# Start of a hybrid decoder block on one core: order of the first loads, of the token scaling and of the first two projection tiles

## Chip, cores and metric

The kernel runs on one core of a Trainium2 chip. The metric is device time in microseconds for one launch; the times of before are three runs. Beside them there is one profiled execution, from which every row below comes. The engines are named as in the profile: PE (TensorE matmul), PEld (its weight load), DVE (VectorE), ACT (ScalarE), POOL (GpSimd) and SP (SyncE, which here only issues DMAs).

## What is computed

16 meta tokens and 256 tokens of width 1024 are layer-normed and projected by `w_in` (1024 x 5640). The columns feed a gated delta net (four heads), a stick-breaking attention (eight heads) and two gates; their outputs are merged, projected, added to the residual and normed; then comes a mixture of 32 experts (one group of four, two experts in it) and a last norm. All of it is float32.

```python
h = layer_norm(jnp.concatenate([meta, x], axis=1), ln_emb_g, ln_emb_b)
proj = h @ w_in                      # (272, 5640)
dn_qkv, dn_z, dn_b, dn_a, sb_qkv, gates = jnp.split(proj, SPLIT_POINTS, axis=-1)
dn_qkv = silu(causal_depthwise_conv(dn_qkv, dn_conv_w))
mix = (sig(gA) * (gated_delta_rule(...) @ w_branch_dn)
       + sig(gB) * (stick_breaking(...) @ w_branch_sb)) @ w_out
h = layer_norm(DEEPNORM_ALPHA * h + mix, ln1_g, ln1_b)
h = layer_norm(DEEPNORM_ALPHA * h + hierarchical_moe(h, ...), ln2_g, ln2_b)
return h[:, N_META:]
```

## The kernel before

**Start of the program.** The meta tokens go to tile `xm` (16 x 1024), the 256 tokens to tile `h1` in two halves of 128 rows (`xt[0]` and `xt[1]`, called first half and second half below; the profile calls both `h`). SP issues these three loads (L112, L113, L115); ACT issues five small parameter loads into `rows` (L114 to L119). While they travel PE runs five matmuls on zeros (L185). For each of the three pieces `norm_stats` (L165) runs two BN_STATS on DVE, then `row_stats` (L172) a BN_AGGR on DVE and two small operations on POOL, an addition and a power (L176, L177), whose result is the row's scale. After all three come three scalings on DVE (L191), in place. Then PE transposes the pieces (L208), 128 columns (one chunk) at a time; each chunk becomes `hf` (272 columns, L211 on ACT or L214 on DVE), a rounded copy `hTh` (L212 on DVE or L215 on ACT) and the rest `hTl` (L216 on DVE). There are eight chunks.

**Projection.** `w_in` is taken in 44 tiles of 128 columns. `load_split` (L224) loads one tile (512 KB, SP, L230) into one of three raw buffers, ACT rounds it (`A.copy`, L231), and POOL, or DVE for three of the tiles, subtracts (L232). Three tiles are kept split (`WB`), and three raw (`WR`). A product is three matmuls (`mm3`, L236 to L238) for each of the eight chunks: high weights by `hTh`, high weights by `hTl`, low weights by `hTh`; the last needs POOL's result.

```python
            c, n0, use, j = todo[i]
            wh, wl = split[i]
            pt = ps("sb" if i % 2 and i < 16 else "acc", f"pj{c}")
            for k in range(KT):
                mm3(pt[:, n0:L], wh[:, k, :], wl[:, k, :], hTh[:, k, n0:], hTl[:, k, n0:], k == 0, k == KT - 1)
            use(pt, j)
```

The first four tiles (columns 512, 640, 768 and 896) are keys: `use` is `conv_use`, ACT's L309, three DVE operations (L311) and ACT's L312. After the fourth tile comes a narrow product `pba`, from which the gating of the delta net is computed on DVE (L417 to L442); PE needs its result at L445.

**What sets the order.** On PE, ACT, DVE and SP a scheduler of the tile framework orders the instructions from their dependences; POOL alone keeps the order in which the code is written (`manual_schedule`). DMAs share eight completion semaphores per kind in turn, so that a DMA also waits until the one that had its semaphore before has landed (the names `DMAHW0` to `DMAHW7` below).

Of the kernel before, what the change touches and what calls it, by code (L numbers as in the profile page):

```python
# [7 lines left out]
F32 = mybir.dt.float32  # L8
# [9 lines left out]
P = 128  # L18
D = 1024
KT = 8  # L20
NM = 16
NT = 256
L = NM + NT
# [13 lines left out]
WR = 3  # L37
# [40 lines left out]
def block_kernel(ctx: ExitStack, tc: tile.TileContext, io, out, dbg=None):  # L78
    nc = tc.nc
    V, A, G, T, S = nc.vector, nc.scalar, nc.gpsimd, nc.tensor, nc.sync  # L80
# [8 lines left out]
    def ps(tag, name):  # L89
        return psp.tile([P, 512], F32, tag=tag, bufs=PB[tag], name=name)  # L90
# [15 lines left out]


# [3 lines left out]
    rows = x0.tile([P, P], F32, name="rows")  # L111
    S.dma_start(xm, io["meta_tokens"])  # L112
    S.dma_start(xt[0], io["x"][:P, :])  # L113
    A.dma_start(rows[0:8, :], io["ln_emb_g"].rearrange("(r p) -> r p", p=P))  # L114
    S.dma_start(xt[1], io["x"][P:, :])  # L115
    A.dma_start(rows[8:16, :], io["ln_emb_b"].rearrange("(r p) -> r p", p=P))
    A.dma_start(rows[16:64, :], io["dn_conv_w"].rearrange("j (r p) -> (j r) p", p=P))
# [68 lines left out]
    xstat = {}  # L186
    for i, xa, n in ((2, xm, NM), (0, xt[0], P), (1, xt[1], P)):
        xstat[i] = norm_stats(xa, n, f"e{i}")
    for i, xa, n in ((2, xm, NM), (0, xt[0], P), (1, xt[1], P)):
        mv, r = xstat[i]  # L190
        V.tensor_scalar(xa[:n], xa[:n], mv[:n, 0:1], r[:n], op0=ALU.subtract, op1=ALU.mult)  # L191
# [30 lines left out]
    wring = []  # L222

    def load_split(src, name, pool=None, bufs=WB, sub=None):  # L224
        a, b = src.shape[1:]
        wring.append(name)
        raw = lt.tile([P, 1024], F32, name=f"wr_{name}", tag=f"wr{len(wring) % WR}").rearrange("p (a b) -> p a b", a=a)
        both = (pool or rg).tile([P, 2048], F32R, name=f"ws_{name}", tag="rd", bufs=bufs)
        wh, wl = (both[:, i * 1024:(i + 1) * 1024].rearrange("p (a b) -> p a b", a=a) for i in range(2))
        S.dma_start(raw, src)  # L230
        A.copy(wh, raw)  # L231
        (sub or V).tensor_sub(wl, raw, f32(wh))  # L232
        return wh, wl
# [6 lines left out]
    w_in = io["w_in"].rearrange("(k p) c -> p k c", p=P)  # L240
# [5 lines left out]
    def project(n):  # L246

        for _ in range(n):
# [4 lines left out]
            c, n0, use, j = todo[i]  # L253
            wh, wl = split[i]
            pt = ps("sb" if i % 2 and i < 16 else "acc", f"pj{c}")
            for k in range(KT):
                mm3(pt[:, n0:L], wh[:, k, :], wl[:, k, :], hTh[:, k, n0:], hTl[:, k, n0:], k == 0, k == KT - 1)
            use(pt, j)
# [1277 lines left out]
```

## Time and profile before

| | us |
|---|---|
| three runs: lowest, median, highest | 559.96, 560.81, 561.68 |
| the profiled execution: own time | 558.53 |
| its span, first to last instruction | 556.8 |
| busy in the span: PE, DVE, ACT, POOL | 475.9, 232.7, 185.0, 171.1 |
| mean granted TensorE clock over the span | 0.937 of full speed |

A span view gives for each engine the time in which it ran something, not the time in which others waited for it. A timeline row gives an instruction's start, its duration, its source line and, in brackets, how long its engine had been idle before it and which event ended that. A duration includes any time that an instruction, once started, was held up.

### The profile page before, as it was taken

To read this page: it belongs to the slowest core of one execution; us is meant where nothing else is said; L and a number is where in the kernel's file an instruction comes from. 1 tells how busy PE (TensorE), PEld (TensorE's weight loads), DVE (VectorE), ACT (ScalarE), POOL (GpSimd) and SP (SyncE) were. 2 spreads that over 40 slices of the span, in tenths; PEclk is the share of its full clock that TensorE was granted. 3 is DMA by queue.
4 is the path that set the end of the run, shared out by engine and by line. 5 is a ranking of instruction groups with operands and counts; after the bars stand their busy time and mean duration, and the time that the engine had idled before them with its cause. 6 is when DMAs were issued, how large, how long until landed. Compare 5 with 4: busy or idle time off the path is not lost. (4 is left out here: it accounts for less than half of the span.)

```text
span 556.8 us, 8809 instructions
## 1 busy us (share of the span) xinstructions
PE 475.9 (85%) x3353; PEld 339.4 (61%) x3353; DVE 232.7 (42%) x516; ACT 185.0 (33%) x382; POOL 171.1 (31%) x154
## 2 busy tenths in 40 slices
PE   7898799999998998999799879886879898468681
PEld 4797788899987876789787755441222233222520
DVE  5785825663245433336995756220120101001016
ACT  2554345446545464444353412120210201101100
POOL 7492886745544355445450300000000000000002
PEclk9698999999999999999999899897999788879796
DMA  8553242233432414339879995999999999999922
GB/s 202 122 141 87 64 120 82 78 89 101 126 103 75 112 43 117 111 99 316 285 276 416 406 395 207 419 417 419 419 420 417 422 419 415 421 403 421 414 115 75
DMA packets 74582, 136.35 MB, mean 245 GB/s; under 512 B 9857, under 2 KB 59154, under 8 KB 62242
## 3 DMA queue, kind: packets, MB, share of 16 engines
q1 hardware_dynamic: 72640, 134.26, 65.5%
q10 hardware_dynamic: 1890, 1.39, 0.7%
q8 instruction: 33, 0.54, 0.4%
q14 instruction: 19, 0.16, 0.1%
HBM read 133.54 MB, written 2.10 MB: 244 GB/s over the span
## 5 line engine op out<-in xcount | busy, mean ns | idle before, releaser
L232 POOL TENSOR_TENSOR ws_in<-wr_in,ws_in 128x1024 fp32r<-128x1024 f32 x41 | 99.1, 2421 | 74.4 <-ACT ws_in L231 71.5
L236 PE MATMUL pj<-hTh,ws_in 128*128 128x256 f32 (+1 forms) x352 | 105.9, 302 | 1.7 <-ACT hTh L215 1.0
L238 PE MATMUL pj<-hTh,ws_in 128*128 128x256 f32 (+1 forms) x352 | 102.5, 292 | 0.0
L237 PE MATMUL pj<-hTl,ws_in 128*128 128x256 f32 (+1 forms) x352 | 102.2, 292 | 0.2 <-DVE hTl L216 0.2
L1273 PE MATMUL pg<-gu,xs 128*32 128x512 f32 x640 | 76.0, 604 | 11.1 <-DMA gu<-expert_w_up 7.7
L1493 POOL TENSOR_SCALAR rs<-mv 128x1 f32<-128x1 f32 x2 | 0.4, 221 | 233.4 <-DVE mv L1492 233.4
L236 PEld LDWEIGHTS pj<-hTh,ws_in 128*128 128x128 f32 x352 | 68.1, 194 | 4.0 <-issue 1.4
L237 PEld LDWEIGHTS pj<-hTl,ws_in 128*128 128x128 f32 x352 | 67.8, 193 | 1.5 <-issue 0.9
L238 PEld LDWEIGHTS pj<-hTh,ws_in 128*128 128x128 f32 x352 | 67.6, 192 | 0.8 <-issue 0.7
L1273 PEld LDWEIGHTS pg<-gu,xs 128*32 128x32 f32 x640 | 32.4, 111 | 50.3 <-issue 44.4
L1322 PE MATMUL py<-dn,hd 128*32 128x512 f32 x320 | 46.8, 717 | 12.8 <-DMA dn<-expert_w_down 7.8
L231 ACT CAST ws_in<-wr_in 128x1024 fp32r<-128x1024 f32 x44 | 45.9, 1042 | 3.1 <-DMA wr_in<-w_in 3.1
L1298 DVE TENSOR_SCALAR sc<-pt,smod 128x256 fp32r<-128x256 f32 x10 | 4.8, 484 | 99.0 <-PE pt L1297 99.0
L1326 DVE TENSOR_TENSOR yy<-py,yy 128x512 fp32r<-128x512 f32 x20 | 13.8, 692 | 63.6 <-ACT yy L1325 56.5
L1322 PEld LDWEIGHTS py<-dn,hd 128*32 128x32 f32 x320 | 10.9, 126 | 39.8 <-issue 24.2
L1334 PE MATMUL y<-yy,sc 128*128 128x512 f32 x80 | 25.8, 439 | 4.3 <-ACT yy L1325 3.0
L1304 ACT ACTIVATE gs<-pg 128x256 f32<-128x256 f32 x10 | 3.8, 384 | 76.4 <-PE pg L1273 76.4
L1334 PEld LDWEIGHTS y<-yy,sc 128*128 128x128 f32 x80 | 13.9, 194 | 21.9 <-ACT yy L1325 7.4
L1325 ACT CAST yy<-py 128x512 fp32r<-128x512 f32 x20 | 11.7, 586 | 45.5 <-PE py L1322 44.4
L729 DVE TENSOR_TENSOR_SCAN kp<-kp,one 128x144 f32<-128x144 f32 (+1 forms) x16 | 17.5, 1125 | 14.8 <-ACT kp L724 14.8
L311 DVE SCALAR_TENSOR_TENSOR qkv<-pj,cols,qkv 128x271 f32<-128x271 f32 (+2 forms) x36 | 17.8, 498 | 12.9 <-ACT qkv L309 12.3
L888 POOL TENSOR_TENSOR h<-h,gb 128x512 f32<-128x512 f32 x8 | 12.9, 1645 | 12.9 <-ACT gb L885 12.9
(539 smaller groups left out, 830.1 us busy)
## 6 DMA issues: line engine op xcount, KB each, us to landing
gu<-expert_w_gate SPq DMA_DIRECT2D x32, 1024.0 KB
gu<-expert_w_up SPq DMA_DIRECT2D x32, 1024.0 KB
dn<-expert_w_down SPq DMA_DIRECT2D x32, 1024.0 KB
wr_in<-w_in SPq DMA_DIRECT2D x44, 512.0 KB
wr_o<-w_out SPq DMA_DIRECT2D x8, 512.0 KB
wr_w_branch_dn<-w_branch_dn SPq DMA_DIRECT2D x4, 512.0 KB
wr_w_branch_sb<-w_branch_sb SPq DMA_DIRECT2D x4, 512.0 KB
h<-x SPq DMA_DIRECT2D x2, 512.0 KB
```

The source lines that it names most:

```text
L231: A.copy(wh, raw)
L232: (sub or V).tensor_sub(wl, raw, f32(wh))
L236: T.matmul(pt, lh, rh, start=first, stop=False)
L237: T.matmul(pt, lh, rl, start=False, stop=False)
L238: T.matmul(pt, ll, rh, start=False, stop=last)
L311: V.scalar_tensor_tensor(y[:, s:], pt[:, :L - s], ccol(3 - s, r + j), y[:, s:], op0=ALU.mult, op1=ALU.add)
L729: V.tensor_tensor_scan(k_, k_, bc(one1, [P, n]), 1.0, op0=ALU.mult, op1=ALU.mult)
L888: G.tensor_tensor(x_, x_, gb, op=op)
L1273: T.matmul(pgd[u, part][c, :], xsd[u, part][:, k, c], raw[e][0][:, :, k, :], start=k == 0, stop=k == KT - 1)
L1322: T.matmul(py[c, :], hd[(u + part) % 2][:, r, c], raw[e][1][:, r, n * 512:(n + 1) * 512], start=r == 0, stop=r == 1)
L1326: V.tensor_sub(yy[:, 1, :], py, f32(yy[:, 0, :]))
L1334: T.matmul(y[t][n], sct[(u + part) % 2][:, t * P:(t + 1) * P], yy[:, p_, :], start=False, stop=p_ == 1 and part == 0 and u == NQ - 1)
```

## The change

The loads of the first three `w_in` tiles are written ahead of three of the small parameter loads (`prefetch`), with `raw_weights` split off from `load_split`. The order of SP's first loads becomes first half of the tokens, meta tokens, second half. The scaling of each piece is written directly behind its own statistics. The first two tiles of the projection are written as one loop over the chunks with three matmuls for each of the two, and both `use` calls behind it. Line numbers grow by 11 to 16 at the start of the program.

```diff
+    def raw_weights(src, name):
+        wring.append(name)
+        a = src.shape[1]
+        raw = lt.tile([P, 1024], F32, name=f"wr_{name}", tag=f"wr{len(wring) % WR}").rearrange("p (a b) -> p a b", a=a)
+        S.dma_start(raw, src)
+        return raw
...
+    def prefetch():
+        there.extend(raw_weights(w_in[:, :, 512 + i * P:512 + (i + 1) * P], f"in{512 + i * P}") for i in range(WR))
...
+    S.dma_start(xt[0], io["x"][:P, :])
     S.dma_start(xm, io["meta_tokens"])
-    S.dma_start(xt[0], io["x"][:P, :])
+    S.dma_start(xt[1], io["x"][P:, :])
     A.dma_start(rows[0:8, :], io["ln_emb_g"].rearrange("(r p) -> r p", p=P))
-    S.dma_start(xt[1], io["x"][P:, :])
     A.dma_start(rows[8:16, :], io["ln_emb_b"].rearrange("(r p) -> r p", p=P))
+    prefetch()
...
-    xstat = {}
     for i, xa, n in ((2, xm, NM), (0, xt[0], P), (1, xt[1], P)):
-        xstat[i] = norm_stats(xa, n, f"e{i}")
-    for i, xa, n in ((2, xm, NM), (0, xt[0], P), (1, xt[1], P)):
-        mv, r = xstat[i]
+        mv, r = norm_stats(xa, n, f"e{i}")
         V.tensor_scalar(xa[:n], xa[:n], mv[:n, 0:1], r[:n], op0=ALU.subtract, op1=ALU.mult)
...
-        wring.append(name)
-        raw = lt.tile([P, 1024], F32, name=f"wr_{name}", tag=f"wr{len(wring) % WR}").rearrange("p (a b) -> p a b", a=a)
+        raw = there.pop(0) if there else raw_weights(src, name)
...
-        S.dma_start(raw, src)
...
-            c, n0, use, j = todo[i]
-            wh, wl = split[i]
-            pt = ps("sb" if i % 2 and i < 16 else "acc", f"pj{c}")
+            tiles = ((0, 1), (), *([j] for j in range(2, len(todo))))[i]
+            pts = [ps("sb" if i % 2 and i < 16 else "acc", f"pj{todo[i][0]}") for i in tiles]
             for k in range(KT):
-                mm3(pt[:, n0:L], wh[:, k, :], wl[:, k, :], hTh[:, k, n0:], hTl[:, k, n0:], k == 0, k == KT - 1)
-            use(pt, j)
+                for i, pt in zip(tiles, pts):
+                    (wh, wl), n0 = split[i], todo[i][1]
+                    mm3(pt[:, n0:L], wh[:, k, :], wl[:, k, :], hTh[:, k, n0:], hTl[:, k, n0:], k == 0, k == KT - 1)
+            for i, pt in zip(tiles, pts):
+                todo[i][2](pt, todo[i][3])
```

The scheduler makes the following of it. Instructions are the same in number and kind on every engine; what differs is their order and what some of them wait for.

SP at the start of the program, before (`wr_in512` is the raw tile of columns 512 to 639, and so on; a bracket names the semaphores waited for):

```order
L112 DMA xm_86<-meta_tokens 16x1024
L113 DMA h1_85<-x 128x1024
L115 DMA h1_85<-x 128x1024
L230 DMA wr_in512_278<-w_in 128x8x128 [waits DMAHW2_49]
L230 DMA wr_in640_283<-w_in 128x8x128 [waits DMAHW4_49]
L230 DMA wr_in768_288<-w_in 128x8x128 [waits DMAHW5_49]
```

SP at the same place in the changed kernel:

```order
L127 DMA h1_85<-x 128x1024
L128 DMA xm_86<-meta_tokens 16x1024
L129 DMA h1_85<-x 128x1024
L113 DMA wr_in512_93<-w_in 128x8x128 [waits DMAHW2_49]
L113 DMA wr_in640_95<-w_in 128x8x128 [waits DMAHW4_49]
L113 DMA wr_in768_97<-w_in 128x8x128 [waits DMAHW5_49]
```

The first two loads have changed places. The three `w_in` loads stood right behind the tokens already; the first of them waits for `DMAHW2`, which is the semaphore of the first half before and of the meta tokens now.

DVE's statistics and scalings, before (`e2` is the meta tokens, `e0` the first half, `e1` the second):

```order
L169 BN_STATS st_e2_144<-xm_86 16x6 [waits DMAHW0_49]
L169 BN_STATS st_e2_144<-xm_86 16x6
L174 BN_AGGR mv_e2_147<-st_e2_144 16x2 [waits DVE_49]
L169 BN_STATS st_e0_152<-h1_85 128x6 [waits DMAHW2_49]
L169 BN_STATS st_e0_152<-h1_85 128x6
L174 BN_AGGR mv_e0_155<-st_e0_152 128x2 [waits DVE_49]
L169 BN_STATS st_e1_160<-h1_85 128x6 [waits DMAHW6_49]
L169 BN_STATS st_e1_160<-h1_85 128x6
L174 BN_AGGR mv_e1_163<-st_e1_160 128x2 [waits DVE_49]
L191 TENSOR_SCALAR xm_86<-xm_86,mv_e2_147,rs_e2_149 16x1024 [waits Pool_49]
L191 TENSOR_SCALAR h1_85<-h1_85,mv_e0_155,rs_e0_157 128x1024 [waits Pool_49]
```

DVE at the same place in the changed kernel:

```order
L185 BN_STATS st_e2_150<-xm_86 16x6 [waits DMAHW2_49]
L185 BN_STATS st_e2_150<-xm_86 16x6
L185 BN_STATS st_e0_159<-h1_85 128x6 [waits DMAHW0_49]
L190 BN_AGGR mv_e2_153<-st_e2_150 16x2 [waits DVE_49]
L185 BN_STATS st_e0_159<-h1_85 128x6
L185 BN_STATS st_e1_168<-h1_85 128x6 [waits DMAHW6_49]
L190 BN_AGGR mv_e0_162<-st_e0_159 128x2 [waits DVE_49]
L185 BN_STATS st_e1_168<-h1_85 128x6
L190 BN_AGGR mv_e1_171<-st_e1_168 128x2 [waits DVE_49]
L204 TENSOR_SCALAR xm_86<-xm_86,mv_e2_153,rs_e2_155 16x1024 [waits Pool_49]
L204 TENSOR_SCALAR h1_85<-h1_85,mv_e0_162,rs_e0_164 128x1024 [waits Pool_49]
```

The meta tokens' statistics still come first, and the three scalings still stand behind all statistics; the semaphores show which load each waits for.

PE at the first chunk, before (`pj512` and `pj640` are the outputs of the first two tiles; `DVE` waits stand for the next chunk's `hTh` and `hTl`, `Pool` waits for the subtracted weights):

```order
L238 MATMUL pj512_293<-hTh_175,ws_in512_279 128x272 [waits Pool_49]
L236 MATMUL pj512_293<-hTh_175,ws_in512_279 128x272 [waits DVE_49]
L236 MATMUL pj640_331<-hTh_175,ws_in640_284 128x272 [waits Activation_49]
L237 MATMUL pj640_331<-hTl_176,ws_in640_284 128x272
L237 MATMUL pj512_293<-hTl_176,ws_in512_279 128x272 [waits DVE_49]
L238 MATMUL pj512_293<-hTh_175,ws_in512_279 128x272
L236 MATMUL pj512_293<-hTh_175,ws_in512_279 128x272 [waits DVE_49]
```

PE there in the changed kernel:

```order
L247 MATMUL pj512_293<-hTh_181,ws_in512_284 128x272 [waits Pool_49]
L245 MATMUL pj640_294<-hTh_181,ws_in640_287 128x272 [waits Activation_49]
L246 MATMUL pj640_294<-hTl_182,ws_in640_287 128x272
L247 MATMUL pj640_294<-hTh_181,ws_in640_287 128x272 [waits Pool_49]
L245 MATMUL pj512_293<-hTh_181,ws_in512_284 128x272 [waits DVE_49]
L246 MATMUL pj512_293<-hTl_182,ws_in512_284 128x272 [waits DVE_49]
L247 MATMUL pj512_293<-hTh_181,ws_in512_284 128x272
```

Three matmuls of tile 640, those of its first chunk, now stand ahead of the second chunk's wait. At the other end of the pair the last matmul of tile 512 was followed by twelve of tile 640 before, and is followed by three now; what stands behind the pair is the same. Of ACT's list two of the later L312 change places; POOL's list is the same.

## Rows read from the trace of the kernel before

**Rows 1.** Windows: us, busy us (instructions) of PE, PEld, DVE, ACT, POOL, PEclk, DMA, GB/s.
```profile
18.46:22.70 4.24, 4.24 (x18) 4.24 (x19) 4.18 (x13) 2.02 (x4) 0.60 (x2) 0.50 0.88 171
22.70:29.00 6.30, 6.30 (x51) 6.30 (x51) 4.18 (x13) 3.28 (x5) 2.51 (x2) 1.00 0.09 8
...
400.00:500.00 100.00, 79.14 (x524) 29.55 (x516) 14.76 (x30) 14.13 (x31) 0.00 (x0) 0.88 1.01 417
```

**Rows 2.** Timeline of PE: start us, us, line, out<-in, [idle before <-releaser].
```profile
18.46 0.82 PE L236 MATMUL pj<-hTh,ws_in 128*128 128x272 f32 x2 [0.71 <-DVE hTh L212]
...
29.27 0.29 PE L238 MATMUL pj<-hTh,ws_in 128*128 128x272 f32 x1
...
45.30 0.39 PE L445 MATMUL pdc<-gg,le 128*128 128x8 f32 x2 [2.62 <-DVE gg L442]
```

**Rows 3.** Timeline of SP's DMA issues at the start of the program.
```profile
0.80 0.40 SPq L112 DMA_DIRECT2D xm<-meta_tokens  x1
1.26 0.41 SPq L113 DMA_DIRECT2D h<-x  x1
...
5.25 2.64 SPq L230 DMA_DIRECT2D wr_in<-w_in  x3
```

**Rows 4.** DMA view, 0 to 10 us: GB/s in slices of 0.25 us.
```profile
GB/s 0 0 0 0 0 0 0 178 101 33 147 98 328 346 354 410 344 332 420 465 377 442 226 97 56 28 4 61 242 244 231 303 342 336 326 334 342 322 309 303
```

**Rows 5.** Timeline of DVE, same columns.
```profile
2.90 1.27 DVE L169 BATCH_NORM_STATS2 st_e<-xm 16x6 f32<-16x512 f32 x2 [1.33 <-DMA xm<-meta_tokens]
...
5.26 1.29 DVE L169 BATCH_NORM_STATS2 st_e<-h 128x6 f32<-128x512 f32 x2 [0.86 <-DMA h<-x]
...
8.03 0.21 DVE L174 BATCH_NORM_AGGREGATE mv_e<-st_e 128x2 f32<-128x12 f32 x1
8.16 0.75 DVE L191 TENSOR_SCALAR xm<-xm,mv_e,rs_e 16x1024 f32<-16x1024 f32 x1
8.83 0.80 DVE L191 TENSOR_SCALAR h<-h,mv_e,rs_e 128x1024 f32<-128x1024 f32 x1
10.40 0.81 DVE L191 TENSOR_SCALAR h<-h,mv_e,rs_e 128x1024 f32<-128x1024 f32 x1 [0.78 <-POOL rs_e L177]
...
15.08 0.96 DVE L216 TENSOR_TENSOR hTl<-hf,hTh 128x272 fp32r<-128x272 f32 x1 [2.30 <-ACT hTh L215]
15.96 2.44 DVE L212 CAST hTh<-hf 128x272 fp32r<-128x272 f32 x1
```

**Rows 6.** Timeline of POOL, same columns.
```profile
8.33 1.38 POOL L176 TENSOR_SCALAR rs_e<-mv_e 128x1 f32<-128x1 f32 x1 [0.57 <-DVE mv_e L174]
9.80 0.57 POOL L177 TENSOR_TENSOR rs_e<-rs_e,mhalf 128x1 f32<-128x1 f32 x1
10.81 7.43 POOL L232 TENSOR_TENSOR ws_in<-wr_in,ws_in 128x1024 fp32r<-128x1024 f32 x3 [0.45 <-ACT ws_in L231]
...
26.49 2.40 POOL L232 TENSOR_TENSOR ws_in<-wr_in,ws_in 128x1024 fp32r<-128x1024 f32 x1 [7.30 <-ACT ws_in L231]
```

**Rows 7.** Timeline of ACT, same columns.
```profile
9.69 1.04 ACT L231 CAST ws_in<-wr_in 128x1024 fp32r<-128x1024 f32 x1 [1.19 <-DMA wr_in<-w_in]
...
13.68 1.05 ACT L231 CAST ws_in<-wr_in 128x1024 fp32r<-128x1024 f32 x1 [1.12 <-DMA wr_in<-w_in]
14.63 0.41 ACT L215 CAST hTh<-hf 128x272 fp32r<-128x272 f32 x1
...
24.98 0.49 ACT L309 ACTIVATE qkv<-pj,cols 128x272 f32<-128x272 f32 x1 [3.34 <-PE pj L238]
```

**Rows 8.** POOL and DVE near 172 us; last, the two L678 together (ns min/median/max).
```profile
171.90 1.01 POOL L677 TENSOR_TENSOR sso<-sso,mhalf 128x4 f32<-128x4 f32 x1 [6.11 <-DVE sso L676]
172.88 2.36 POOL L232 TENSOR_TENSOR ws_in<-wr_in,ws_in 128x1024 fp32r<-128x1024 f32 x1
...
172.94 2.32 DVE L678 TENSOR_TENSOR sso<-sso,rq 128x4 f32<-128x4 f32 x1 [1.18 <-POOL sso L677]
...
L678 DVE TENSOR_TENSOR sso<-sso,rq x2: 165/1242/2319, 172.9 to 204.2; 128x4 f32<-128x4 f32 x2
```

More of the change, by code (lines that the diff above doesn't have):

```diff
@@ L105, in block_kernel @@
     x0 = x0_cm.__enter__()
+    wring, there = [], []
+    def raw_weights(src, name):
[4 more added lines that the diff above has]
+        return raw
+    w_in = io["w_in"].rearrange("(k p) c -> p k c", p=P)
+    def prefetch():
+        there.extend(raw_weights(w_in[:, :, 512 + i * P:512 + (i + 1) * P], f"in{512 + i * P}") for i in range(WR))
     hx = pools["hx"].tile([P, 2048], F32, name="h1", tag="rd", bufs=1).rearrange("p (t d) -> p t d", t=2)
@@ L219, in block_kernel @@
     mx = gs_cm.__enter__()
-    wring = []
     def load_split(src, name, pool=None, bufs=WB, sub=None):
         a, b = src.shape[1:]
-        wring.append(name)
-        raw = lt.tile([P, 1024], F32, name=f"wr_{name}", tag=f"wr{len(wring) % WR}").rearrange("p (a b) -> p a b", a=a)
+        raw = there.pop(0) if there else raw_weights(src, name)
         both = (pool or rg).tile([P, 2048], F32R, name=f"ws_{name}", tag="rd", bufs=bufs)
         wh, wl = (both[:, i * 1024:(i + 1) * 1024].rearrange("p (a b) -> p a b", a=a) for i in range(2))
-        S.dma_start(raw, src)
         A.copy(wh, raw)
@@ L238, in mm3 @@
         T.matmul(pt, ll, rh, start=False, stop=last)
-    w_in = io["w_in"].rearrange("(k p) c -> p k c", p=P)
     todo, split = [], []
```

## Prediction

> **What bounds the kernel now.** The windows come first. From 400 to 500 us the DMA engines are full (share 1.01 at 417 GB/s) and PE runs 79 of 100 us; that is the stream of expert weights [rows 1], which the change leaves alone. The change lies wholly in the first 30 us, so the question is how late the projection gets going there, and whether that lateness travels to the end. PE's timeline answers the second half: at 45.30 PE has waited 2.62 us for the gating, which is computed from the product behind the fourth tile [rows 2]. What moves the first four tiles moves this wait with it. Everything later hangs on PE or on buffers that PE frees, so I let a shift pass to the end one for one; the bounds are no shift at the end and all of it.
>
> The first half is a chain to be followed by hand. PE starts to run without a gap at 18.46, released by DVE's L212, the rounded second chunk [rows 2]. That instruction started at 15.96 and took 2.44 us [rows 5], while POOL ran its three weight subtractions from 10.81 to 18.24 [rows 6]: DVE was held up until POOL was through. So POOL's third subtraction sets PE's start, not the loads and not the statistics. POOL in turn came to its first subtraction at 10.81, after ACT's first rounding (9.69, 1.04 us) [rows 7] and after its own power operation for the second half, which ended at 9.80 + 0.57 = 10.37 [rows 6].
>
> **The first loads.** The first half is now issued first, 1.26 - 0.80 = 0.46 us earlier [rows 3]. Its statistics began on landing at 5.26 [rows 5], so it should land near 4.80. The meta tokens are issued behind it on the same queue. The DMA view shows the two halves as one block of traffic from 3.00 on, at about 350 GB/s [rows 4]; if the queue keeps its order, the 64 KB of meta tokens follow 0.19 us behind the first half, and land near 4.95 where they landed at 2.90 [rows 5]. Two things wait for them now: DVE's first statistics, and the first `w_in` load, which stands right behind on SP and was released at 5.25 by the first half [rows 3]. It goes 0.3 us earlier. The three tiles then land 0.3 us earlier, which frees ACT from 13.68 + 1.05 = 14.73 to about 14.4 [rows 7]; the small loads on ACT's queue are in nobody's way. That is the whole gain of the early loads, and it is not on the chain.
>
> **The statistics.** DVE's order is the same; only its start is late. Six BN_STATS at 0.64 us (1.27 for two) and two BN_AGGR at about 0.13 (8.03 - 5.26 is four of the one and one of the other) [rows 5] put the last BN_AGGR at 4.95 + 6 x 0.64 + 2 x 0.13 = 9.05, against 8.03. This is 1.0 us late, because before DVE did the meta tokens while the first half was still on its way. The scalings are no nearer to their statistics than before.
>
> **POOL's scale.** Before, POOL's addition for the second half started at 8.33 and took 1.38 us, since DVE's two scalings ran from 8.16 to 9.63 [rows 5, 6]. Now DVE's scalings come behind POOL's power for the first half. That power starts 0.6 us after the second BN_AGGR (at 8.3), so it lasts until 9.45; the scalings take 1.47 as before, to 10.9; the addition gets in at 11.0, and the power of the second half ends at 11.65 instead of 10.37. That is 1.3 us late. If the scalings needn't wait for POOL's power, it is 1.0.
>
> **The subtractions.** The first rounding is done near 10.4, so POOL needs to wait for nothing and goes straight from the power into the first subtraction. DVE's scaling of the second half waits for the same power. The trace has this case once: at 171.90 POOL ran such a power and at 172.88 a subtraction; DVE's L678, which waited for the power, started at 172.94 and took 2.32 us, where the other L678 took 0.165 [rows 8]. So I take the scaling as held up until 11.65 + 2.36 = 14.0. It then takes some 0.7 us from POOL. Before, the scaling was done at 11.21 and cost POOL little. POOL's end is then 11.65 + 3 x 2.36 + 0.7, plus 0.1 for L216, which gets in between the second and the third as it did at 15.08 [rows 5]: 19.55 against 18.24, 1.3 us late. If DVE's scaling starts first, POOL waits the same 0.7 and the end is the same. The scaling reads one SBUF tensor, L678 reads two; that one input is enough is shown by L212, a CAST with 2.44 us [rows 5]. [...]
>
> Meanwhile the second half's transposes come 3 us later than they did, but the rounded first chunk left ACT only at 14.63 + 0.41 [rows 7], so PE's first product is about 1 us late, and still ahead of POOL's end. Bounds of this term: nothing (the chain of before) and 2.4 us (the scaling is passed over by a second subtraction as well).
>
> **The pair of tiles.** Three matmuls of tile 640 now run ahead of the second chunk's wait, in a gap that stood idle for 0.71 us [rows 2]. In the stretch that follows a matmul takes 4.24 / 18 = 0.24 us, at the lower clock level, 1.2 GHz (granted 0.50) [rows 1]: 0.7 us saved, of which 0.1 goes because the next product then waits for the second chunk's `hTl`. Against it, the last matmul of tile 512 stands nine places later, at 6.30 / 51 = 0.124 us each (2.4 GHz) [rows 1]: 1.1 us. ACT is in order there: L309 for tile 512 at 24.98 [rows 7], behind it the rounding of tile 896, then POOL's subtraction, done at 26.49 + 2.40 = 28.89 [rows 6]. PE's first matmul that needs it ran at 29.27 [rows 2], so 0.4 us of cover stood there. Nine places use it up: 0.7 us is given back. The pair is worth -0.6 + 0.7 = +0.1 us. The conv operations of both tiles (L311) have the time of the third tile to run in; the two small DVE products that moved ahead of them sit in idle time, and cost nothing unless the third tile starts late too.
>
> **Sum.** +1.35 (L212 from 18.40 to 19.75) + 0.1 = +1.45 us. The profiled execution's 558.53 becomes 560.0. That execution is 2.3 us below the median of the three runs and below the lowest, so I carry the difference to the median: 560.81 + 1.45, **562.3 us**. A measurement of this kernel can tell about 0.3% from no change, which is 1.7 us.
>
> **The rivals.**
> *The meta tokens do not queue (no change).* Then they land 2.1 us after their issue, as before (2.90 - 0.80 [rows 3, 5]), near 3.4, DVE does them ahead of the first half, and `w_in` starts right behind the second half. The last BN_AGGR comes at 7.6 and the power ends at 10.0. POOL runs 10.0 + 7.1 + 0.8 = 17.9, so PE starts 0.3 us early: 560.81 - 0.3 + 0.1, 560.6. For it: the small transfer had its data in half a microsecond [rows 4]. Against it: one queue, and the block of traffic. [...]
> *The clock comes back early (faster).* From 18.46 to 22.70 PE ran at 1.2 GHz [rows 1]. If the pair's three matmuls and the fuller stretch bring 2.4 GHz at PE's start, half of 4.24 us is saved: -2.1. On top of the rival above that is 558.5; on top of the forecast, 560.2. It decides from the point where PE starts no later than 18.9. Against it: PE idles longer ahead of that stretch, since the transposes of the first half start 1.3 us later.
> *Passed over twice (slower).* L212, standing right behind L216, lost to POOL's third subtraction [rows 5, 6]. If the second half's scaling loses to two subtractions, it ends at 17.1, the first chunk is ready at 18.5, and L212 at 20.4: +2.0 + 0.1, 562.9. A clock that comes back 1 us later than it did behind PE's start adds 0.5 to any case.
> *Nothing arrives.* The shift is absorbed before the experts: 560.8.
>
> **Chances.** Forecast 0.45, spread from 561.2 to 563.4; meta tokens early 0.18; clock early 0.15; passed over twice, or the forecast with a late clock, 0.15; absorbed 0.07. Of the forecast's own spread 0.2 lies above +1.7 us and 0.25 below it. Slower by over 0.3%: 0.2 + 0.14 = 0.34. Within 0.3%: 0.25 + 0.18 + 0.07 = 0.50, with 0.01 of the late clock. Faster: 0.15. The range must reach the early meta tokens and the twice passed: 559.0 to 563.7; what is left out is most of the early clock and the worst of the late one.
>
> **What would show it.** Right: the meta tokens' statistics near 5 us, the last BN_AGGR near 9, the second half's L191 with a duration over 2 us beside POOL's first subtraction, POOL's third done near 19.5, L212 ending just behind it; and PE idle for some 0.7 us in front of the fourth tile's low-weight product, waiting for POOL. Wrong: statistics before 4 us (the queue), a normal L191 of 0.8 us and POOL done by 18.3 (the lock), a granted clock of 1.00 before 21 us, or PE's wait at the gating no later than 45.3 with the same end.

## The result, and the profile after

The change made the kernel slower: **564.88 us** (median of 13 runs, 561.15 to 567.58) against 560.16 us (13 runs, 558.46 to 561.68), a ratio of 1.0078 with a 95% interval of 1.0057 to 1.0100. That is +4.7 us, where +1.45 was forecast, and above the range. All ratios in this document leave out runs over 1.5% above the fastest of their kernel, which the medians include, so a ratio need not be that of the medians beside it.

The profiled execution of the changed kernel took 566.19 us (span 564.5), that of before 558.53 (span 556.8): 7.7 us apart, more than the medians, and that execution of before lies 1.6 us under its own median. So the two traces show places; what a part costs is taken from medians, further down. The same instruction, in both traces:

| instruction | before, us | after, us | later by |
|---|---|---|---|
| ACT's first rounding of `w_in` | 9.69 | 10.69 | 1.00 |
| POOL's subtraction for the fourth tile | 26.49 | 28.07 | 1.58 |
| gating's products on PE | 45.30 | 46.99 | 1.69 |
| PE's first product for the small inversion (`i0m`) | 65.49 | 68.59 | 3.10 |
| a product of the output projection | 300.00 | 304.11 | 4.11 |
| gate of the last expert group but one (ACT, L1304, now L1315) | 509.21 | 515.52 | 6.31 |
| its last `down` result (ACT, L1325, now L1336) | 515.32 | 523.32 | 8.00 |
| gate of the last group | 536.94 | 544.61 | 7.67 |

At the gating it is as late as forecast. Three jumps follow: behind the gating, behind `i0m`, and behind 500 us.

The start first. Timelines of SP's issues, of DVE, of POOL and of ACT in the changed kernel, with the columns of the rows of before (start us, us, line, what, [idle before <-releaser]); they answer to [rows 3], [rows 5], [rows 6] and [rows 7]:

```profile
0.80 0.40 SPq L127 DMA_DIRECT2D h<-x  x1
1.25 0.42 SPq L128 DMA_DIRECT2D xm<-meta_tokens  x1
...
4.66 3.93 SPq L113 DMA_DIRECT2D wr_in<-w_in  x3
```
```profile
4.67 1.27 DVE L185 BATCH_NORM_STATS2 st_e<-xm 16x6 f32<-16x512 f32 x2 [3.11 <-DMA xm<-meta_tokens]
...
8.49 0.21 DVE L190 BATCH_NORM_AGGREGATE mv_e<-st_e 128x2 f32<-128x12 f32 x1
8.62 0.75 DVE L204 TENSOR_SCALAR xm<-xm,mv_e,rs_e 16x1024 f32<-16x1024 f32 x1
9.44 1.71 DVE L204 TENSOR_SCALAR h<-h,mv_e,rs_e 128x1024 f32<-128x1024 f32 x2
...
16.71 2.49 DVE L225 CAST hTh<-hf 128x272 fp32r<-128x272 f32 x1
```
```profile
9.53 0.77 POOL L193 TENSOR_TENSOR rs_e<-rs_e,mhalf 128x1 f32<-128x1 f32 x1
11.81 7.19 POOL L241 TENSOR_TENSOR ws_in<-wr_in,ws_in 128x1024 fp32r<-128x1024 f32 x3 [1.51 <-ACT ws_in L240]
...
28.07 2.39 POOL L241 TENSOR_TENSOR ws_in<-wr_in,ws_in 128x1024 fp32r<-128x1024 f32 x1 [8.35 <-ACT ws_in L240]
```
```profile
10.69 1.05 ACT L240 CAST ws_in<-wr_in 128x1024 fp32r<-128x1024 f32 x1 [1.91 <-DMA wr_in<-w_in]
...
26.56 0.49 ACT L320 ACTIVATE qkv<-pj,cols 128x272 f32<-128x272 f32 x1 [4.13 <-PE pj L247]
```

The meta tokens queue behind the first half (4.67). DVE's scalings are through at 11.15, before POOL's first subtraction starts at 11.81; POOL waits 1.51 us for ACT, and ACT 1.91 us for `w_in`. So not POOL's power but the landing of `w_in` makes POOL late here: its third subtraction ends at 11.81 + 7.19 = 19.00, against 18.24 before.

PE's timeline, answering to [rows 2]: the wait for the fourth tile's low weights, that for the gating, and that for `i0m`.

```profile
30.51 0.39 PE L247 MATMUL pj<-hTh,ws_in 128*128 128x272 f32 x1 [0.64 <-POOL ws_in L241]
...
46.99 0.47 PE L456 MATMUL pdc<-gg,le 128*128 128x8 f32 x2 [2.96 <-DVE gg L453]
...
68.59 0.28 PE L482 MATMUL i0m<-ident,pTm 64*64 64x64 f32 x1 [3.25 <-DVE pTm L479]
```

What follows the gating is seen in windows of 2 us (columns as in [rows 1]; PEclk is the third number from the end). First the changed kernel, then before:

```profile
44.00:46.00 2.00, 0.03 (x1) 0.00 (x0) 1.90 (x4) 0.41 (x1) 1.93 (x3) 1.00 0.12 28
46.00:48.00 2.00, 1.01 (x6) 1.01 (x6) 1.49 (x6) 0.00 (x0) 0.63 (x3) 0.79 0.69 176
48.00:50.00 2.00, 2.00 (x11) 1.96 (x11) 1.13 (x2) 0.24 (x2) 0.00 (x0) 0.50 0.29 86
50.00:52.00 2.00, 2.00 (x11) 1.81 (x11) 0.36 (x2) 0.00 (x0) 0.00 (x0) 0.50 0.21 36
52.00:54.00 2.00, 2.00 (x11) 1.94 (x11) 0.90 (x2) 0.60 (x1) 0.00 (x0) 0.50 0.76 226
54.00:56.00 2.00, 2.00 (x20) 1.97 (x19) 0.39 (x1) 1.32 (x2) 0.00 (x0) 1.00 0.00 0
```
```profile
46.00:48.00 2.00, 2.00 (x13) 1.90 (x13) 1.40 (x3) 0.24 (x2) 0.00 (x0) 0.66 0.41 123
48.00:50.00 2.00, 2.00 (x11) 1.81 (x11) 0.09 (x1) 0.10 (x1) 0.00 (x0) 0.50 0.33 81
50.00:52.00 2.00, 2.00 (x18) 1.97 (x18) 1.29 (x2) 1.23 (x3) 0.00 (x0) 0.99 0.60 181
```

Behind the wait PE falls to half its clock (granted 0.50) in both: before from 46.6 to 50.0 us, now from 47.2 to 54.0. PE is busy all the while, so the longer stretch is time lost: the lateness grows from 1.69 to 3.10 us by `i0m`. Behind `i0m` the same: 67.1 to 70.5 before, 67.7 to 74.5 now, another 1.0 us.

In the expert stage it is again the level. PE's products there, first before, then changed, then two windows of the changed kernel:

```profile
502.15 7.03 PE L1273 MATMUL pg<-gu,xs 128*32 128x512 f32 x58 [2.77 <-DMA gu<-expert_w_up]
...
511.61 3.64 PE L1322 MATMUL py<-dn,hd 128*32 128x512 f32 x32 [0.51 <-ACT hd L1313]
```
```profile
506.76 8.72 PE L1284 MATMUL pg<-gu,xs 128*32 128x512 f32 x58 [3.15 <-DMA gu<-expert_w_up]
...
517.92 5.34 PE L1333 MATMUL py<-dn,hd 128*32 128x512 f32 x32 [0.51 <-ACT hd L1324]
```
```profile
508.00:511.00 3.00, 3.00 (x20) 1.08 (x16) 0.00 (x0) 0.00 (x0) 0.00 (x0) 0.50 1.00 418
...
518.00:521.50 3.50, 3.50 (x20) 0.94 (x24) 0.00 (x0) 0.93 (x3) 0.00 (x0) 0.53 1.02 421
```

The same 58 products take 8.72 instead of 7.03 us, the 32 behind them 5.34 instead of 3.64. The buffers of the last experts come free with the 58 products, so the loads into them start late too: SP issues the next `gu` at 509.30 before and at 515.61 now, each 0.1 us behind the 58.

### The profile page after: what moved, and what is told of

Read it like the earlier page. It is cut to its first block, busy times and chain, and to the rows that moved or that the text cites. A ratio compares the mean times of both kernels' runs of the same rounds, so it can differ in the third digit from the quotient of the medians.

```text
span 564.5 us, 8808 instructions
## 1 busy us (share of the span) xinstructions
PE 481.9 (85%) x3353; PEld 341.9 (61%) x3353; DVE 232.4 (41%) x516; ACT 184.7 (33%) x382; POOL 170.9 (30%) x154
## 5 line engine op out<-in xcount | busy, mean ns | idle before, releaser
L246 PE MATMUL pj<-hTl,ws_in 128*128 128x256 f32 (+1 forms) x352 | 103.5, 295 | 0.4 <-DVE hTl L229 0.4
L1284 PE MATMUL pg<-gu,xs 128*32 128x512 f32 x640 | 77.5, 614 | 11.6 <-DMA gu<-expert_w_up 8.0
L245 PEld LDWEIGHTS pj<-hTh,ws_in 128*128 128x128 f32 x352 | 68.9, 197 | 3.2 <-issue 1.4
L247 PEld LDWEIGHTS pj<-hTh,ws_in 128*128 128x128 f32 x352 | 68.6, 195 | 1.7 <-POOL ws_in L241 0.9
L1333 PE MATMUL py<-dn,hd 128*32 128x512 f32 x320 | 48.0, 733 | 13.1 <-DMA dn<-expert_w_down 8.1
L1315 ACT ACTIVATE gs<-pg 128x256 f32<-128x256 f32 x10 | 3.8, 383 | 78.1 <-PE pg L1284 78.1
L1336 ACT CAST yy<-py 128x512 fp32r<-128x512 f32 x20 | 11.7, 586 | 47.0 <-PE py L1333 45.9
```

Source lines behind the costliest of these rows:

```text
L245: T.matmul(pt, lh, rh, start=first, stop=False)
L246: T.matmul(pt, lh, rl, start=False, stop=False)
L247: T.matmul(pt, ll, rh, start=False, stop=last)
L1284: T.matmul(pgd[u, part][c, :], xsd[u, part][:, k, c], raw[e][0][:, :, k, :], start=k == 0, stop=k == KT - 1)
L1333: T.matmul(py[c, :], hd[(u + part) % 2][:, r, c], raw[e][1][:, r, n * 512:(n + 1) * 512], start=r == 0, stop=r == 1)
```

## The experiments

Every ratio is to the kernel before on the same chip; its medians there were 559.5 to 560.3 us.

**Which part costs.** The change, taken apart.

*First half ahead of the meta tokens, nothing else:*
```diff
-    S.dma_start(xm, io["meta_tokens"])
     S.dma_start(xt[0], io["x"][:P, :])
+    S.dma_start(xm, io["meta_tokens"])
```


> The kernel before with one part of the change: first half ahead of the meta tokens in SP's queue (everything else as before, statistics all ahead of the scalings, tiles one by one). Theory (wba's load, which waits for the first load of SP's queue to be done, now goes out beside the w_in loads and slows them): the first rounding of w_in near 10.7 us as in the changed kernel (9.69 before), POOL's third subtraction ends 0.7 to 1 us late, the gating's products 0.7 to 1.2 us late. Rival (the lateness comes from the scalings or the pair): first rounding by 9.7, gating within 0.3 us of before. The time: the lateness and up to 3.4 us of half level, so +1 to +4.5; it says little by itself.

560.43 us (10 runs), ratio 1.0005 (0.9975 to 1.0035). First rounding at 9.49: `w_in` was not late in this execution, against the theory on `wba`. The gating came 1.1 us late all the same. DVE and POOL of this run:
```profile
9.10 0.21 DVE L174 BATCH_NORM_AGGREGATE mv_e<-st_e 128x2 f32<-128x12 f32 x1
...
10.05 3.58 DVE L191 TENSOR_SCALAR h<-h,mv_e,rs_e 128x1024 f32<-128x1024 f32 x2
```
```profile
10.68 2.40 POOL L232 TENSOR_TENSOR ws_in<-wr_in,ws_in 128x1024 fp32r<-128x1024 f32 x1
...
13.46 4.91 POOL L232 TENSOR_TENSOR ws_in<-wr_in,ws_in 128x1024 fp32r<-128x1024 f32 x2 [0.38 <-ACT ws_in L231]
```
The last BN_AGGR at 9.10 (forecast 9.05), and the two scalings together 3.58 us instead of 0.80 + 0.81 [rows 5]: the second was held until POOL's first subtraction was over at 13.08. That far it is the prediction's chain, but POOL itself was not late: its power for the second half was done by 10.7 (forecast 11.65), and the third subtraction ended at 13.46 + 4.91 = 18.37 (forecast 19.55, before 18.24). PE started 0.16 us late:
```profile
18.62 0.82 PE L236 MATMUL pj<-hTh,ws_in 128*128 128x272 f32 x2 [0.76 <-DVE hTh L212]
```
Most of the 1.1 us comes from the clock. PE is busy all through here, first in this run, then in before (columns as in [rows 1]):
```profile
22.70:24.70 2.00, 2.00 (x11) 2.00 (x11) 1.25 (x5) 0.00 (x0) 0.00 (x0) 0.50 0.28 16
```
```profile
22.70:24.70 2.00, 2.00 (x17) 2.00 (x17) 1.12 (x4) 0.00 (x0) 0.00 (x0) 0.99 0.23 14
```
With 11 products there instead of 17, PE is 1.0 us late at 25 us. The return to the full clock (granted 1.00), at 24.8 here, stood at 22.8 to 25.1 in the eight executions with the first half ahead, and at 21.4 to 23.9 in the twelve with the old order.

*The two tiles side by side, nothing else* (the change's lines in `project`), twice:

> The kernel before with another part alone: the first two tiles of the projection side by side. Theory: PE fills 0.6 us of its gap with the second tile, POOL's subtraction for the fourth tile starts 0.5 to 0.8 us late (26.49 before), PE waits for it, and the gating's products are between 0.3 us early and 0.5 us late. Rival (the pair carries most of the lateness): 1 us late or more.

> The kernel before with the pair alone, once more, for more executions (four counted the first time, 563.3 to 565.0). Theory A: the gating is only 0.4 us late, so most executions lie lower than those four, median 561 to 562.5. Theory B: again 563.5 to 565.

564.19 us (4 runs), ratio 1.0084 (1.0051 to 1.0117); then 563.28 us (12 runs), ratio 1.0052 (1.0017 to 1.0087). The pair alone costs 3 to 4 us: nearer to theory B, and theory A was wrong about the median. Yet its direct lateness, 0.44 us at the gating and 0.52 in the repeat, is small. PE and the windows of the first of the two runs:
```profile
45.74 0.59 PE L447 MATMUL pdc<-gg,le 128*128 128x8 f32 x2 [2.79 <-DVE gg L444]
```
```profile
44.00:46.00 2.00, 0.26 (x2) 0.26 (x2) 1.73 (x9) 0.00 (x0) 1.31 (x5) 0.84 0.31 57
46.00:48.00 2.00, 2.00 (x10) 1.96 (x11) 0.66 (x3) 0.24 (x2) 0.00 (x0) 0.50 0.70 205
...
52.00:54.00 2.00, 2.00 (x19) 1.99 (x17) 1.27 (x2) 0.95 (x2) 0.00 (x0) 0.95 0.18 52
```
The gating's products start at the half level, which lasts until 52.2 us. The two profiles flatter the pair a little: at the start of the projection the level came back at 21.5 and 21.4, where it took until 22.7 in before. Half of 1.3 us, some 0.6, is my estimate of what that hides.

*Scalings behind their statistics, nothing else* (the change's lines in the loop over the three pieces):

> The kernel before with the third part alone: each piece scaled right behind its statistics, loads in the old order. Theory: scalings sooner, last BN_AGGR later by the scalings in front of it (up to 0.8 us), POOL's power for the second half done by 10.4 to 11, still about when the first rounding is done; the gating's products within 0.4 us of before. Rival: POOL's power pushes the subtractions, 1 us late or more.

560.07 us (10 runs), ratio 1.0007 (0.9985 to 1.0029); gating at 45.22. Neither a cost nor a gain can be told.

*The changed kernel with its tiles one by one:*
```diff
-            tiles = ((0, 1), (), *([j] for j in range(2, len(todo))))[i]
...
+            for k in range(KT):
+                mm3(pt[:, n0:L], wh[:, k, :], wl[:, k, :], hTh[:, k, n0:], hTl[:, k, n0:], k == 0, k == KT - 1)
+            use(pt, j)
```


> The changed kernel with its tiles one by one again (loads and scalings stay as changed). Theory A (lateness sets how often the clock drops at the waits): the fourth tile's low weights no longer late, PE does not wait for POOL behind 29 us, the gating's products at 46.0 to 46.4 (46.99 in the changed kernel), 561 to 563 us, between before and after. Theory B (the pair itself sets it, as the run with the pair alone stood at 564): within 1 us of before.

559.98 us (12 runs), ratio 0.9997 (0.9966 to 1.0029): theory B. The gating is late here by 1.32 us and the median is that of before. Its PE and windows:
```profile
46.62 0.39 PE L453 MATMUL pdc<-gg,le 128*128 128x8 f32 x2 [2.70 <-DVE gg L450]
```
```profile
48.00:50.00 2.00, 2.00 (x14) 1.81 (x13) 1.41 (x3) 0.00 (x0) 0.00 (x0) 0.60 0.09 27
50.00:52.00 2.00, 2.00 (x12) 1.94 (x11) 0.51 (x1) 0.60 (x1) 0.00 (x0) 0.55 0.74 185
52.00:54.00 2.00, 2.00 (x20) 1.98 (x19) 0.78 (x2) 1.32 (x2) 0.00 (x0) 1.00 0.26 77
```
The level falls late, at 48.4, and is back at 51.8. (This profiled execution, 563.81 us, is the longest of the twelve; more on that below.)

*Only the second tile's first three products ahead* (put into the kernel before, into the changed kernel, and into the kernel before with the new scalings):
```diff
-            for k in range(KT):
-                for i, pt in zip(tiles, pts):
+            for k, i, pt in sorted([(k, i, pt) for k in range(KT) for i, pt in zip(tiles, pts)], key=lambda q: (q[0] > 0, q[1], q[0])):
```


> The kernel before with the second tile's first three products alone moved ahead, into PE's gap; behind them tile 512 is finished, then tile 640. What the pair gains is kept and what it loses is not: the dense stretch 0.6 us shorter, POOL's subtraction for the fourth tile within 0.4 us of 26.49, no wait of PE for it, the gating's products 0.1 to 0.6 us earlier than before. Theory A: 0 to 0.6 us faster than before, not measurably. Theory B (any side-by-side order costs): slower, 562 or more.

> The changed kernel with the second tile's first three products alone moved ahead (as in the run that did this to the kernel before); loads and scalings stay as changed. Theory: no wait of PE for POOL behind 29 us, the gating's products 0.4 to 0.6 us earlier than in the changed kernel, the stretch behind the gating 3.4 us: 559 to 561, like the change without the pair. Rival (the late loads cost too, once PE's order is new): 562 or more.

> The kernel before with the two harmless parts: scalings behind their statistics and the second tile's first three products ahead; loads in the old order. Theory: gating 0.1 to 0.6 us earlier than before, 559 to 560, ratio 0.996 to 1.000. Rival: as before, 560.

559.10 us (12 runs), ratio 0.9989 (0.9961 to 1.0016); 561.01 us (12 runs), ratio 1.0012 (0.9982 to 1.0042); 559.98 us (12 runs), ratio 1.0002 (0.9972 to 1.0032). As theory A expected: with tile 512 finished first, no loss can be told. In the first of them POOL and PE stand thus:
```profile
26.40 2.40 POOL L232 TENSOR_TENSOR ws_in<-wr_in,ws_in 128x1024 fp32r<-128x1024 f32 x1 [7.25 <-ACT ws_in L231]
```
```profile
45.20 0.39 PE L447 MATMUL pdc<-gg,le 128*128 128x8 f32 x2 [2.60 <-DVE gg L444]
```
The gating gains 0.1 us. Its median is the lowest of all, but none of the three can be told from before.

*The small loads out of the way, and the changed kernel once more:*
```diff
-    A.dma_start(wba, io["w_in"][:, 2048:2056].rearrange("(k p) c -> p k c", p=P))
+    S.dma_start(wba, io["w_in"][:, 2048:2056].rearrange("(k p) c -> p k c", p=P))
```
(`alog` and `dtb` likewise.)

> The changed kernel with the loads of wba, alog and dtb issued on SP's queue behind the three w_in loads, no longer on ACT's queue beside them. Theory: w_in lands where it would without them, first rounding at 9.7 or earlier (10.69 in the changed kernel), POOL's third subtraction ends by 18.3 (19.0), the gating's products 0.6 to 1.0 us earlier than in the changed kernel. Rival (something else delays w_in, the meta tokens or the prefetch's place): first rounding stays near 10.7.

> The changed kernel unchanged, beside the others on one chip. Both theories: 564 to 565 us. Its profile tells whether the two longer stretches at the half level (behind the gating and behind i0m) and the two more behind 500 us come again in another execution: by theory A some of them do, not necessarily all.

562.26 us (10 runs), ratio 1.0025 (0.9992 to 1.0059), so the first of the two can't be told from before; and 565.48 us (9 runs), ratio 1.0091 (1.0058 to 1.0125). The first rounding stood at 9.99 in the one, but at 9.93 in the unchanged repeat too, and at 11.00 in a run with the old loads (the first row with the new scalings). So this landing moves by over 1 us from execution to execution, and the 1.00 us of the table above is not shown to be the change's. It leans that way: the median is 10.69 in the seven executions with all of the new loads, 9.9 in the twelve with the old ones. Whether `wba` has part in it is not decided.

The repeat's profile (562.22 us) shows what the expert stage is worth. At 493 us it is 3.9 us behind before, the first profile of the changed kernel 4.5; at the end 3.7 against 7.7. In the repeat the products behind 500 us took the times of before, 7.03 and 3.64 us, where before was granted 1.00 from 500 to 520 us:
```profile
506.28 7.03 PE L1284 MATMUL pg<-gu,xs 128*32 128x512 f32 x58 [3.17 <-DMA gu<-expert_w_up]
...
515.74 3.64 PE L1333 MATMUL py<-dn,hd 128*32 128x512 f32 x32 [0.51 <-ACT hd L1324]
```

**Does the wait make the cost?** Kernels that move or fill PE's waits.

*Extra products in the third tile* (7, and 15):
```diff
+            for _ in range(7 if i == 2 else 0):
+                T.matmul(pt[:, 272:], wh[:, 7, :], hTl[:, 7, 32:], start=True, stop=True)
             for k in range(KT):
```


> The kernel before, with seven extra products of 240 columns in the third tile of the projection (into columns of the bank that nobody reads): PE and all behind it 7 x 0.115 = 0.8 us late, nothing else changed. Clock theory (the half-level stretches behind PE's two waits, at the gating and at i0m, get longer when the waits move): +0.8 us and, if a stretch lengthens, 1.0 to 1.7 us more for each. Rival (the extra time belongs to the change's own lateness on POOL, ACT and DVE): +0.8 us and the two stretches as before, 3.4 us each.

> The same with fifteen extra products: 15 x 0.115 = 1.7 us of delay, as much as the change's at the gating. Clock theory: +1.7 us, and with it the longer half-level stretches that the changed kernel shows (6.8 us each), +3.4 to +5 in all, though loads, statistics, scalings and tiles are those of before. Rival: +1.7 us at most, stretches of 3.4 us.

563.75 us (7 runs, 558.32 to 567.05), ratio 1.0048 (1.0010 to 1.0087); 562.30 us (12 runs, 559.51 to 569.01), ratio 1.0034 (1.0008 to 1.0060). Neither was the pure delay that was meant: PE's wait went elsewhere (1.2 us for the transposes of `baT`, the narrow product's result, in the one; 1.4 us left at the gating in the other), and in both profiles the stretch behind the gating was gone (in the first it stood at 38.8 to 42.2 us instead). Both profiles were ahead of before at `i0m`, by 0.9 and 0.7 us, where they were meant to be behind. So they don't tell which theory holds. They do show that the pair is not the only change of PE's order that can cost 2 to 4 us in the median.

*Both waits filled with projection*, in the kernel before and in the changed one:
```diff
+    def decays():
         pdc = ps("gd", "pdc")
...
         gating()
         yield
+        yield
+        decays()
...
+        yield
         p0 = pst("i0")
```


> The kernel before with the gating's products emitted one step of the weave later and the inversions one step more: useful products of the projection run in PE's two waits (15 more before the gating's products: 1.8 of the 2.62 us; some 48 more before i0m, all of the 3.25 us). Clock theory: PE is hardly idle, no half-level stretch behind 24 us in the first 100 us; up to 5 us of idle time and up to 3 us of half level saved, unless the inversions, now later, wait elsewhere: -3 to -8 us. Rival (the level falls for another reason, or the chain of the inversions bounds the stage): the stretches stay, -2 to +2 us.

> The changed kernel with the same two waits filled. Clock theory: no half-level stretch behind 24 us in the first 100 us here either, so it stands only its late start above the run with the waits filled and the loads of before: +1.3 to +1.7 us between the two, where the pair before and after stood 4.7 us apart. Rival (the extra belongs to the change itself): the distance stays near 4.7 us.

563.41 us (12 runs), ratio 1.0050 (1.0021 to 1.0079), and 563.05 us (12 runs), ratio 1.0069 (1.0042 to 1.0096). Filling didn't pay: the projection ran 12 us ahead of before around 100 us and was level with it again by 220 us (the recurrence, issued later, may hold that stage; this wasn't tried). The distance between loads and tiles of before and of after, 4.7 us with the waits open, is smaller: nothing by the medians, 1.1 us by the ratios, whose intervals leave some 2 us either way. Both kernels are some 3 us above before, though, so something else may hide it. In the two profiles it is 1.3 us at 220 to 300 us. The window behind `i0m`, the kernel before with waits filled, then the changed one:
```profile
64.00:76.00 12.00, 12.00 (x93) 11.37 (x93) 6.01 (x10) 5.17 (x10) 9.76 (x8) 1.00 0.50 131
```
```profile
64.00:76.00 12.00, 12.00 (x95) 11.57 (x95) 5.30 (x13) 4.52 (x9) 8.32 (x6) 1.00 0.36 89
```
Both are granted 1.00 there; the changed one had one short stretch at 60 us (0.79 granted in the mean of 56 to 64 us).

*Small products in the wait at the gating*, with the pair and without:
```diff
         pdc = ps("gd", "pdc")
+        for _ in range(8):
+            T.matmul(pdc[:, 256:264], ones, z2[:, :8], start=True, stop=True)
```


> The kernel before with the pair alone, and eight small products (8 columns, into columns that nobody reads) ahead of the third tile behind the fourth: some 8 x 0.22 = 1.8 us of PE's wait at the gating (2.8 to 2.9 us with the pair) are taken by them, for 0.24 us of projection that moves behind. Clock theory: if these products hold the level, the stretch behind the gating is 3.4 us or gone, and the median falls from 563.3 to 564.2 to 561 to 562; if they don't hold it, the level falls as before and nothing is gained. Rival (the late weights cost by themselves): 563 to 564.5 with the stretch shortened.

> The kernel before with the same eight small products and no pair: the wait of 2.62 us shrinks to some 0.8. Clock theory: if they hold the level, no stretch behind the gating: 1 to 1.5 us faster, 558.5 to 559; if not, 560. Rival: 560, whatever the level does.

563.79 us (12 runs, 558.71 to 569.65), ratio 1.0051 (1.0016 to 1.0087), and 563.91 us (12 runs, 559.53 to 569.54), ratio 1.0047 (1.0012 to 1.0083). Against the clock theory: with the pair, the profiled execution had no stretch at either wait and took 558.7, and yet the median stayed. But the same products cost as much without the pair (3.9 us by the medians, 2.6 by the ratio), and they changed PE's order behind the gating. So this pair of runs decides nothing.

**Where the cost arises.** Both kernels, ended behind the projection, the recurrence and the stick-breaking:
```diff
     gs_cm.__exit__(None, None, None)
     ht_cm.__exit__(None, None, None)
+    for t in range(2):
+        S.dma_start(out[t * P:(t + 1) * P, :], xt[t])
+    br_cm.__exit__(None, None, None)
+    psp_cm.__exit__(None, None, None)
+    return
```


> The kernel before, ending behind the projection, the recurrence and the stick-breaking: the branch products, the router and the experts are left out, and the scaled tokens are written to the output. Every engine's order is that of before up to there. It ends near 250 us. Both theories: this is the zero of the comparison with the next run; its own scatter tells how much of the 6 us of scatter of the whole kernel arises in the first part.

> The changed kernel, cut at the same place (branch products, router and experts left out). Front theory (lateness of 1.3 to 1.7 us and the longer stretches at the two waits make the difference): 3 to 4.5 us above the run before it. Rival (the expert stage makes it, out of a start that is a little late): 1 to 2 us above it, and the rest of the 4.7 us arises behind 250 us.

257.81 us (6 runs, 254.45 to 259.23) and 260.16 us (5 runs, 259.23 to 261.00): 2.35 us between the medians, and 3.35 if the two longest runs of the first kernel (259.10 and 259.23) are left out. With so few runs this can't tell the two theories apart: between half and some 70% of the 4.7 us has arisen at 250 us, the rest arises in the stages behind. Of the kernel's scatter, nearly 5 us show in the first part alone.

## Why the prediction was wrong

*The meta tokens queue: right.* Forecast 4.95, seen 4.67, on the heels of the first half (a load of ACT's that waits for the first half goes out at 4.41). In this execution the two loads landed in the order of their issue (0.80 and 1.25).

*`w_in` 0.3 us earlier: issued, not landed.* Its first load went out 0.6 us earlier (4.66 against 5.25), but the landing scatters by more than that (first rounding 9.49 to 11.45 over all profiles) and was rather later than earlier.

*The statistics, and the scaling that POOL passes over: seen with the new order of loads alone, absent in the changed kernel's profile.* In that run the last BN_AGGR stood at 9.10, and the scaling took some 2 us more than before. In the changed kernel the meta tokens landed 0.6 us earlier than in that run (4.67 against 5.28) and `w_in` 1.2 us later, so scaling and subtraction did not meet.

*POOL's power and the subtractions: wrong.* The forecast put POOL's addition for the second half behind DVE's scalings of the meta tokens and of the first half. In both profiles it came in between these two, at 8.85 in the changed kernel and 9.46 with the new order of loads alone, and the power was done near 10.3 and 10.7, not at 11.65. POOL's third subtraction ended at 19.00 and 18.37, where 19.55 was forecast. With the new order alone it was the late return to the full clock (granted 1.00 from 24.8 us), which the forecast had as a rival worth 0.5 us, that made most of the gating's lateness.

*The pair's own lateness: the wait was right, the net too low.* PE waited 0.64 to 0.66 us for the fourth tile's low weights in all six profiles with the full pair and open waits (0.7 forecast). With the pair alone the gating was 0.44 and 0.52 us late, not 0.1, although the level had come back early. The forecast's two levels are the granted 0.50 and 1.00 of the profile: in before a product of 272 columns starts 0.227 us behind the last one at the first (20 to 22.6 us) and 0.126 us behind it at the second (23.5 to 29 us), in the changed kernel likewise.

*The sum at the gating: near, in part by luck.* +1.69 us in the profile, +1.45 forecast. Of it L212 makes 0.8 us (its end 19.20 against 18.40; 1.35 forecast), and by the landing of `w_in`, not by POOL's power; the rest came with the pair and with the level, which was back 0.5 us later than in before.

*"The pair is worth +0.1 us" and "I let a shift pass to the end one for one": this step failed.* The price of a part is not its lateness at the next wait. The lateness of 1.1 to 1.3 us at the gating that the new loads bring without the pair left no mark in the median (ratios 1.0005 and 0.9997, with intervals that still admit 1.3 us). The pair, 0.4 to 0.5 us late, cost 3 to 4 us. Within these intervals all of the loss hangs on the pair: every kernel with the full pair and open waits had a higher median (562.3 to 565.5, the lowest of them not clear of noise), every one that has the pair's first row, or none, and PE's order otherwise unchanged lay between 559.1 and 561.0.

*What carries the loss.* The profiles suggest one carrier: the half-level stretches behind PE's waits and in the expert stage, which the prediction knew only as a late return at the start. At the gating, in fourteen executions with that wait open:

| kernel | PE's wait, us | level falls, after PE's restart, us | at granted 0.50, us |
|---|---|---|---|
| before | 2.62 | 1.3 | 3.4 |
| scalings only | 2.63 | 1.3 | 3.4 |
| first row | 2.60 | 1.5 | 3.4 |
| front, before | 2.70 | 1.5 | 3.4 |
| load order only | 2.75 | 2.2 | 3.4 |
| change without the pair | 2.70 | 1.8 | 3.4 |
| change with the first row | 2.60 | 2.2 | 3.4 |
| first row and scalings | 2.67 | 0.5 | 6.8 |
| changed kernel, `wba` late | 2.88 | 1.4 | 3.4 |
| front, changed | 2.94 | 0.8 | 3.4 |
| changed kernel | 2.96 | 0.2 | 6.8 |
| changed kernel again | 2.76 | 0.5 | 6.8 |
| pair only | 2.79 | -0.4 | 6.8 |
| pair only again | 2.87 | -0.6 | 6.8 |

Where the level fell about when PE restarted, the stretch was 6.8 us, and by `i0m` PE was 1.1 to 1.4 us later than it had been at the gating; where it fell 0.8 us behind the restart or later, the stretch was 3.4 us and the lateness stayed within 0.1 us. With the pair the wait is longer each time (2.76 to 2.96 us against 2.60 to 2.75), and four of six stretches were long, against one of eight. That the pair *makes* long stretches more frequent is what these fourteen suggest; it is not shown, since each is one execution. Behind `i0m` the pair makes no such difference: long in three of the six, and in four of the eight.

The expert stage has two outcomes too. Of the eighteen profiles of whole kernels, six show further half-level stretches between 503 and 522 us; these six took 563.8 to 566.2 us and lost 3.0 to 5.7 us from 493 us to the end, compared with before. The twelve others took 558.2 to 562.2 us and moved there by -0.3 to +1.1. Three of the six have no pair (the change without the pair, fifteen extra products, small products without the pair). So among the profiles these stretches go with the long times.

How often an execution takes that long is told by all the times measured. Above 563 us, a line between these two groups of profiles, lie 30 of 48 executions with the full pair and open waits, 5 of 68 with the pair's first row or none and the waits open, and 15 of 133 of before, run beside them. That the pair makes such executions more frequent is thus shown; that it does so through the stretches is not, since a kernel has only one or two profiled executions. The mean granted clock is known of every run, and leans the same way: 0.932 to 0.936 in the changed kernel and the pair alone, 0.938 in before, but 0.938 also with `wba` late. Over the span this is 3 to 8 us more at the half level, of which PE, if busy all the while, loses half: 1.4 to 3.8 us by this estimate, of a loss of 3 to 5.

*What stays open.* 1.3 us in four cases of six, against one of eight, is 0.7 us, and with the pair's 0.4 to 0.5 that is 1.1 to 1.2 of the 2.35 to 3.35 us found in the first part. Behind 250 us, if every time above 563 us stood for the late stretches, 3.2 us in 30 of 48 cases against 5 of 68 would be 1.8 us; that is an estimate from times alone. Why the pair, a few tenths late at the gating, should bring those late stretches is not explained: before 493 us the one profile without the pair that has them and open waits (the change without the pair) was no later than others without them. Nor is the run with small products, whose median stayed high while its profiled execution showed no stretch at either wait. Some profiles have stretches at 310 to 340 us as well, with and without the pair.

## What to carry to other kernels

A change that moved a wait of the busiest engine by 0.4 to 0.5 us cost 3 to 4 us here; so a shift found at the next wait is the least sure term of a sum, and what the engine's level does behind each wait (here 3.4 or 6.8 us at granted 0.50) should stand in the range. Finish the tile whose result another engine is waiting for: running two tiles side by side for the sake of one short gap delayed the first result by nine products, and moving only the three products that fit into the gap had no cost that could be told. Where a kernel's own runs scatter over 6 us or more, parts must be tried one by one and over ten or more executions, since a single profile of the slower kernel may well be the faster one (558.7 us, in a kernel with a median of 563.8).

## What the hardware showed unexpectedly

The level of TensorE's clock, granted 0.50 or 1.00, did not change at the same places of the program in these executions. Its first rise in the span stood at 5.7 us in before, 6.2 and 6.0 in two executions of the changed kernel, 7.8 and 7.7 in two of the pair alone, and 4.6 to 7.7 in the others. Later changes moved with it: behind the gating the level fell 41.0 us after that first rise in eleven of the fourteen executions of the table, while PE's restart lay anywhere from 45.2 to 47.2 us (37.5 in the two of the pair alone, 44.4 in the changed kernel's front). What sets the first rise no run shows. A wait of 2.75 us was followed by 3.4 us at granted 0.50 in one execution (the new order of loads alone), and one of 2.76 us by 6.8 in another (the changed kernel again).
